# One decoder trunk on one core: later block products and Gram products, later keys in the last head, held sums and fewer table operations in the first head, closer steps in the last scan

## The chip, the core and the metric

The kernel runs on one NeuronCore of a Trainium2 chip. The core has a matrix engine (TensorE, "PE" in the profile, with its weight loads listed apart as "PEld"), a vector engine (VectorE, "DVE"), a scalar engine (ScalarE, "ACT"), a general engine (GpSimd, "POOL") and a queue engine (SyncE, "SP") that only issues transfers. Each engine works through its own instructions in order and waits for the others by semaphores. Transfers (DMA) are issued from the queues of SP, ACT and POOL and run beside the engines. The metric is the time of one execution in microseconds (us).

## The reference

Two residual layers over 512 positions of width 2048, in float32. Layer 0 is gated differential attention (8 heads, two query/key pairs of 128 and a value of 256 each, RMS norm and rotary positions on queries and keys). Layer 1 is an RWKV-7 time mixing with 32 heads of 64.

```python
proj = h @ w_in                                      # layer 0: q, k, v, gate
q = apply_rope(rms_norm(q, q_gain), cos, sin)
k = apply_rope(rms_norm(k, k_gain), cos, sin)
a = softmax(q1 k1) - lam * softmax(q2 k2)            # causal
o = rms_norm(a @ v, subln_w) * (1.0 - lambda_init)
x = x + (o * silu(gate)) @ w_out
...
def step(S, inp):                                    # layer 1: the scan over time
    r_t, w_t, k_t, v_t, a_t, b_t = inp
    sa = jnp.einsum('bhvk,bhk->bhv', S, a_t)
    S = S * w_t[:, :, None, :] + sa[..., None] * b_t[:, :, None, :] + v_t[..., None] * k_t[:, :, None, :]
    y = jnp.einsum('bhvk,bhk->bhv', S, r_t)
    return S, y
```

The result of the scan is normalised per head (group norm), gated and projected back.

## The kernel before

**Products and weights.** Every large product is made of three passes over values that are split in a high part and a low rest (`mm3`, L122 of the listing: high x high, high x low, low x high), each a matmul with 512 moving columns. Weights arrive by DMA in blocks of 512 KB (`wraw`, three buffers). `split_w` turns a block into its high part on ACT (`wh`, L105) and its rest on DVE (`wl`, L106), two buffers each. `split_w` is marked urgent: the compiler's list scheduler, which orders each engine's instructions by their place in the program less an offset and by when it thinks that their inputs are ready, puts it ahead of its place (offset `AHEAD`, 2000). `tc.issue_after(ins)` only orders: what is written under it comes behind `ins` on the same engine.

**Chains.** Small work that has to run between the large matmuls is written as generators in `Chain`. Each `yield n` means: go on after n more of the large matmuls. `tick` is called for each of these and counts only for the first chain of the list; a later chain's count starts when the one before has ended. `finish` runs what is left of a chain at once. A chain's steps have an offset of `SCAN` (3000), the solve one of `SOLVE` (4000).

**Layer 0.** The first head's projections are plain (`unit_tok`: 16 rows of blocks in 8 weight blocks, four token tiles; 192 matmuls). From the second head on, `unit_head` needs fewer products by using sums and differences of quarters of the input. `input_sums` makes these sums for eight pairs of input blocks while the first head runs: nine DVE operations and three ACT operations for each pair (L497, L498, L502, L514, L519, L521), written ahead of the first head's second projection, and a last sum (`late`) behind it. The input pairs lie in buffers that are later used for values, gates and the chained weight blocks `Ta` to `Td`. `rope_tables` builds the tables of cosines and sines with the gains, tile by tile (L221 to L225). `attention` is a chain of a head's scores, softmax, weighted values and output transposes; its first step also transposes the keys and queries of the last two token tiles (`turn_qk`, L296). The last head's chain (`rows` is given then) runs under the output projection, a `unit_tok` whose `all_rows` forces the chain to its end before matmul 150; it starts after 16 matmuls.

**Layer 1.** The heads go in 16 pairs, `for j in range(D // P)`. An iteration makes the value projection of pair j (`proj(2, j)`), the key projection of the next pair, from the fourth iteration on a gate projection of an earlier pair, and the next pair's receptance projection; each `proj` is a `unit_chan` of 48 matmuls. In iteration 1 the gate projection of pair 0 stands in the place of the third. After 18 matmuls of `proj(2, j)`, `behind` issues `gram`: the sums of squared keys (L1335) and the 32 Gram products (L1352), their copies on ACT and stores by SP to `ltd`. `t_solve` loads that back through POOL's queue (`LT`) and solves a triangular system row by row on DVE (L1411, L1413), and SP stores the result (`td<-Tm`). Pairs 0 to 2 are solved in one go, 3 to 14 in parts.

The chain of pair j-1 starts at the head of iteration j. `t_combine` loads the solved blocks (`TT<-td`, SP), waits `lead` matmuls, transposes them on DVE (L1450), 8 matmuls later multiplies them with the Gram blocks (the block products, `px`, L1456), 10 later with the other factor (L1467), and 8 later `scan_pair` begins: eight chunks of 64 positions, each with three products (L1549, L1560, L1567) `gap`, `gap` and `gap_s` matmuls apart, ACT's copies between the first two (L1552, L1562), DVE's state update behind the third (L1571). `outputs` (L1589, L1593) and `centre` end it. The bank of `px` is also that of `stage_v`'s product, which `y` (L1482) reads. The lead is 64 for the first chain, 18 for the second, 42 for the third and 10 after that; the gaps are (4, 5) for pairs 0 and 1, (5, 6) for pair 2, (6, 8) for pairs 3 to 13, (4, 4) for pair 14. `group_norm` of pair j-2 (L1615 to L1621) runs ahead of `proj(2, j)` if that pair's chain has ended (`normed`), and otherwise in `behind`, after `t_solve`; `finish_y` (L1628, L1630) turns its result back.

The last pair's chain starts behind the loop, 24 matmuls after the one before has ended, with lead 24 and gaps (5, 5), under two gate projections and the first columns of the output projection; its group norm and `finish_y` are called at matmul 144 of that.

Of the kernel before, what the change touches and what calls it, by code (L numbers as in the profile page):

```python
# [18 lines left out]
ALU = mybir.AluOpType  # L19
# [4 lines left out]
P = 128  # L24
# [3 lines left out]
NT = T // P  # L28
# [58 lines left out]


@urgent
def split_w(g, parts, kg, cols, k0, raw=None, fine=False, turn=None):  # L90

    nc = g.nc
    if raw is None:
        raw = g.wraw.tile([P, kg, cols], F32, name="wraw", tag="wraw")
        if turn:
            g.fetch(k0, kg)
        load_w(g, raw, parts, k0, slice(0, kg))
    hi = g.wh.tile([P, kg, cols], F32R, name="wh", tag="wh")
    lo = g.wl.tile([P, kg, cols], F32R, name="wl", tag="wl")
    for ks in [slice(k, k + 1) for k in range(kg)] if fine else [slice(0, kg)]:  # L100
        k = k0 + ks.start
        with ExitStack() as after:
            for ins in g.made[-1] if turn and g.made else ():
                after.enter_context(g.tc.issue_after(ins))
            a = nc.scalar.copy(hi[:, ks], raw[:, ks])  # L105
            d = nc.vector.tensor_sub(lo[:, ks], raw[:, ks], hi[:, ks].bitcast(F32))  # L106
        if turn:
            turn(ks.stop - ks.start, a.ins, d.ins)
    return hi, lo


# [4 lines left out]
def vg_cols(aps, h):  # L116
    return aps["da_w_in"], 2 * h + 1
# [43 lines left out]
                c.step(g)  # L161


def unit_tok(g, aH, aL, parts, cols, npp=NT, more=None, late=True, turn=None, behind=None):

    nc = g.nc
    pts = [g.pp.tile([P, 512], F32, name="pp", tag="pp") if npp == NT or t % 3 == 0 else
           g.ps.tile([P, 512], F32, name="pt", tag="pb", bufs=2) for t in range(NT)]
    KG = 1024 // cols
    m = None  # L170
    for k0 in range(0, KT, KG):
        raw, fine = g.first.pop(0) if g.first else (None, False)
        wh, wl = split_w(g, parts, KG, cols, k0, raw, fine, turn)
        by_k = fine or more and late and k0 + KG == KT
        order = [(k, t) for k in range(KG) for t in range(NT)] if by_k else \
                [(k, t) for t in range(NT) for k in range(KG)]
        for i, (k, t) in enumerate(order):
            if more and i in (0, 2, 4):
                more(k0 + (k + 1 + i % 4 // 2 if by_k else KG + i // 2), m)
            kk = k0 + k  # L180
            s = slice(t * P, (t + 1) * P)
            with g.tc.issue_after(behind) if behind and not m else ExitStack():
                m = mm3(nc, pts[t][:, :cols], aH[kk][:, s], aL[kk][:, s], wh[:, k, :], wl[:, k, :],
                        kk == 0, kk == KT - 1, g)
    return pts


def rope_tables(g, aps):
    nc = g.nc
    c = g.lc  # L190
    wide = g.work.tile([P, 4, NT, 64], F32, name="rope", tag="sB2", bufs=1)
    ang, n, sn, cs = [wide[:, i] for i in range(4)]
    rows = g.work.tile([P, 4, P], F32, name="ropein", tag="a", bufs=1)
    pos_i = g.small.tile([P, NT], I32, name="pos_i", tag="mx")
    nc.gpsimd.dma_start(out=pos_i[:], in_=aps["positions"].rearrange("o (t p) -> (o p) t", p=P),)
    pos = g.small.tile([P, NT], F32, name="pos", tag="nb")
    nc.vector.tensor_copy(pos[:], pos_i[:])
# [12 lines left out]
    nc.vector.tensor_scalar(ang[:], ang[:], math.pi, -math.pi, ALU.min, ALU.max)  # L210
    nc.scalar.activation(sn[:], ang[:], AF.Sin)
    nc.scalar.activation(cs[:], ang[:], AF.Sin, scale=0.5)
    nc.vector.tensor_mul(cs[:], cs[:], cs[:])
    nc.vector.tensor_scalar(cs[:], cs[:], -2.0, 1.0, ALU.mult, ALU.add)
    g.C = c.tile([P, NT, 2, P], F32, name="ropeC")
    g.S = c.tile([P, NT, 2, P], F32, name="ropeS")
    for i, nm in enumerate(("da_q_gain", "da_k_gain")):
        gn = rows[:, i]
        nc.gpsimd.dma_start(out=gn[:], in_=aps[nm][0].partition_broadcast(P))
        for t in range(NT):  # L220
            nc.vector.tensor_mul(g.C[:, t, i, 0:64], cs[:, t, :], gn[:, 0:64])  # L221
            nc.vector.tensor_mul(g.C[:, t, i, 64:128], cs[:, t, :], gn[:, 64:128])
            nc.vector.scalar_tensor_tensor(g.S[:, t, i, 0:64], sn[:, t, :], -1.0, gn[:, 64:128],
                                           ALU.mult, ALU.mult)
            nc.vector.tensor_mul(g.S[:, t, i, 64:128], sn[:, t, :], gn[:, 0:64])  # L225


def lambda_full(g, aps):
# [98 lines left out]
def attention(g, h, qkT, qkL, sq, V, VL, G, gap, rows=None, keys=()):  # L327
# [92 lines left out]
    for i in range(NT + 3):  # L420
# [12 lines left out]
        if i < NT:  # L433
            scores(i)
        if i == 0 and keys:
            yield 7
            turn_qk(*keys[0])
            yield 9
            turn_qk(*keys[1], "pc")
            yield max(gap - 28, 6)  # L440
        else:
            yield gap - 12
# [27 lines left out]
KG = 2  # L470


def input_sums(g, pairs, late):
# [34 lines left out]
    for k in range(NH4):  # L508
# [10 lines left out]
        nc.vector.scalar_tensor_tensor(c, c, norm(k + NH4), d, ALU.mult, ALU.add)  # L519
        put("S4", k, c)  # L520
        nc.vector.tensor_sub(a, a, b)  # L521


def first_tiles(g, aps, h):
# [288 lines left out]
def layer0(g, aps):  # L813
# [3 lines left out]
    with ExitStack() as cx:  # L817
# [95 lines left out]
        for h in range(NH):  # L913
# [15 lines left out]
            else:  # L929
                for ts in ([0, 1], [2, 3]):  # L930
                    head_qk(g, t1s, sq, ts)
                Chain(g, keys(2), 120)
                input_sums(g, pairs, False)
                ps = unit_tok(g, g.hH, g.hL, vg_cols(aps, h), 512)
                acc1 = g.work.tile([P, 2, 512], F32, name="acc1", tag="acc1", bufs=1)
                G, vg = gates(g)
                vg += [acc1[:, 0], acc1[:, 1]]
                copy_out(g, vg, ps)
                for c in list(g.chains):
                    c.finish(g)  # L940
                input_sums(g, pairs, True)
                first_tiles(g, aps, 1)
                values = head_vg(g, h, vg, G)
            before = qkT + (sq,) + values
# [688 lines left out]
def layer1(g, aps):  # L1633
    nc, tc = g.nc, g.tc
    with ExitStack() as cx:
# [6 lines left out]
        def proj(i, j, **k):  # L1642
            return unit_chan(g, (aps["rw_w_in"], i * KT + j), P, **k)[0]
# [24 lines left out]
        for j in range(D // P):  # L1668
            p = pairs[j]
            if j:  # L1670
# [7 lines left out]
                if full:  # L1678
                    others += [(4, lambda p=p: next(p.solve)), (6, lambda p=p: (next(p.solve), weigh()))]
                gaps = ((6, 8) if j > LAG + 1 else (5, 6)) if full else (4, 4) if j > LAG else (4, 5)  # L1680
                leads = {1: 64, LAG: 18, LAG + 1: 42}
                chain(g, j - 1, pairs[j - 1], 5, *gaps, others, leads.get(j, GAP_D - GAP_T)).step(g)
            stage2(g, j, r, p)
            normed = j > LAG + 1 and pairs[j - 2].chain.wait is None
# [14 lines left out]
                if j > 1 and not normed:  # L1699
                    group_norm(g, j - 2, pairs[j - 2])  # L1700

            stage_v(g, j, p, proj(2, j, behind=(18, behind)))
            if j == 0:
                turn_keys(g, p, 0)
                turn_keys(g, p, 4)
# [9 lines left out]
            weigh()  # L1715
            if j == LAG:
                gated(g, 0, pairs[0], first)
        chain(g, j, p, 24, 5, 5, lead=24)
        gps = proj(3, j - 1)
        group_norm(g, j - 1, pairs[j - 1])  # L1720
        gts = [gate(g, j - 1, gps)]
# [139 lines left out]
```

## Time and profile before

| | us |
|---|---|
| median of 3 timed runs | 2065.39 |
| lowest and highest | 2064.68, 2065.81 |
| profiled execution, whole | 2068.84 |
| its span, first to last instruction | 2067.1 |
| PE busy in it | 2047.3 |
| DVE, ACT, POOL busy in it | 1608.3, 1136.2, 387.5 |

The page of the profile gives busy times of each engine and the chain of work that ended last. A list of waits says for which instruction of which line an engine stood idle, and what released it; the name of the releaser is that of the last semaphore event by the profile. A table by windows gives, for any stretch of time, the busy time and count of each engine and the mean granted clock of PE as a share of full speed. The order of time lists single instructions: start, duration, engine, line, operation, what is written from what, count, and in brackets the idle time just before, with its releaser.

### The profile page before, as it was taken

The numbers are of one execution on the slowest core, as the hardware profiler recorded it, in microseconds if no ns is written. First come the engines' busy times: TensorE is split into PE (matmuls) and PEld (weight loads), VectorE is DVE, ScalarE is ACT, GpSimd is POOL, SyncE is SP. The second block draws the span as 40 slices with busy tenths as digits, with TensorE's granted clock in tenths as the row PEclk, the third lists the DMA queues.
The fourth block names the chain that finished last, engine by engine and source line by source line (L and its number), as shares of the span: only waits on it lengthen the run. The fifth ranks groups of instructions, "written<-read, shape, count | busy, mean of one in ns | idle before, by whom it ended". The sixth has DMA issues, their size and how long they took to land.

```text
span 2067.1 us, 34180 instructions
## 1 busy us (share of the span) xinstructions
PE 2047.3 (99%) x11922; PEld 1676.8 (81%) x11922; DVE 1608.3 (78%) x4128; ACT 1136.2 (55%) x2262; POOL 387.5 (19%) x774
## 2 busy tenths in 40 slices
PE   9999999999999999999999999999999999999999
PEld 8788888888888888888777778888888888877787
DVE  7988988888898976476777788877777887767745
ACT  5765656565666544365465555555555555545333
POOL 1020111102011000101132322322222222232011
PEclk9999999999999999999999999999999999999999
DMA  8487978879787965823333223233333233346676
GB/s 286 151 163 193 178 173 184 164 192 165 190 178 171 271 215 173 173 86 107 92 85 95 87 86 96 88 95 98 97 97 98 87 95 87 106 129 198 199 191 143
DMA packets 159533, 297.76 MB, mean 144 GB/s; under 512 B 64528, under 2 KB 81936, under 8 KB 159360
## 3 DMA queue, kind: packets, MB, share of 16 engines
q1 hardware_dynamic: 110768, 184.39, 28.7%
q0 software_dynamic: 25952, 90.88, 23.1%
q10 hardware_dynamic: 22640, 20.30, 3.1%
q8 instruction: 94, 1.54, 0.3%
q14 instruction: 79, 0.65, 0.1%
HBM read 271.33 MB, written 24.18 MB: 143 GB/s over the span
## 4 chain that ended last, share of the span: by engine, by line
PE 85%; DVE 9%; ACT 2%; issue 2%; DMA 1%; ACTq 0%; DVEq 0%; SPq 0%
PE pp L122 44%; PE pp L573 22%; PE pt L122 5%; DVE wl L106 2%; PE sm L1549 2%; PE gp L1352 1%; PE sc L122 1%; PE o L122 1%; PE sm L1567 1%; PE sm L1560 1%; ACT wh L105 1%; PE Y L1589 1%; DVE tmpl L1411 1%; PE lora L1094 1%; PE z L122 1%
## 5 line engine op out<-in xcount | busy, mean ns | idle before, releaser
L106 DVE TENSOR_TENSOR wl<-wraw,wh 128x1024 fp32r<-128x1024 f32 (+1 forms) x286 | 350.6, 1226 | 176.4 <-ACT wh L105 169.5
L105 ACT CAST wh<-wraw 128x1024 fp32r<-128x1024 f32 (+1 forms) x286 | 299.4, 1047 | 250.4 <-PE pp L122 124.8
L122 PE MATMUL pp<-hL,wh 128*128 128x512 f32 x1024 | 415.1, 405 | 0.0
L122 PE MATMUL pp<-hH,wh 128*128 128x512 f32 x1024 | 414.0, 404 | 0.4 <-ACT wh L105 0.4
L122 PE MATMUL pp<-hH,wl 128*128 128x512 f32 x1024 | 414.1, 404 | 0.0
L122 PEld LDWEIGHTS pp<-hH,wh 128*128 128x128 f32 x1024 | 193.6, 189 | 35.4 <-ACT wh L105 0.6
L122 PEld LDWEIGHTS pp<-hL,wh 128*128 128x128 f32 x1024 | 193.6, 189 | 33.8
L122 PEld LDWEIGHTS pp<-hH,wl 128*128 128x128 f32 x1024 | 193.8, 189 | 32.4
L573 PE MATMUL pp<-wh,hH 128*128 128x512 f32 x448 | 176.8, 395 | 0.0
L573 PE MATMUL pp<-wh,hL 128*128 128x512 f32 x448 | 175.7, 392 | 0.0
L122 PE MATMUL pp<-wl,hH 128*128 128x512 f32 x376 | 147.8, 393 | 0.9 <-DVE wl L106 0.9
L122 PE MATMUL pp<-wh,hL 128*128 128x512 f32 x376 | 147.5, 392 | 0.0
L122 PE MATMUL pp<-wh,hH 128*128 128x512 f32 x376 | 147.2, 392 | 0.1
L1411 DVE SCALAR_TENSOR_TENSOR tmpl<-LT,Tm 128x60 f32<-128x60 f32 (+24 forms) x496 | 134.4, 271 | 13.3
L573 PE MATMUL pp<-wl,hH 128*128 128x512 f32 x448 | 140.4, 392 | 0.0
L1555 POOL COPY SA<-VS 64x64 f32<-64x64 f32 x224 | 57.0, 254 | 405.3 <-DVE VS L1571 383.4
L1413 DVE TENSOR_TENSOR Tm<-Tm,tmpl 128x60 f32<-128x60 f32 (+24 forms) x496 | 104.2, 210 | 11.7
L1552 ACT COPY rhs<-sm 64x64 f32<-64x64 f32 x256 | 53.0, 207 | 92.2 <-PE sm L1549 89.6
L573 PEld LDWEIGHTS pp<-wl,hH 128*128 128x128 f32 x448 | 84.4, 188 | 17.2
L573 PEld LDWEIGHTS pp<-wh,hH 128*128 128x128 f32 x448 | 84.2, 188 | 17.3 <-issue 0.3
L573 PEld LDWEIGHTS pp<-wh,hL 128*128 128x128 f32 x448 | 84.2, 188 | 16.3
L1562 ACT COPY VS<-sm 64x64 f32<-64x64 f32 x256 | 52.9, 207 | 72.9 <-PE sm L1560 66.4
(432 smaller groups left out, 4378.1 us busy)
## 6 DMA issues: line engine op xcount, KB each, us to landing
wraw<-in_rw_w_in_dram SPq DMA_DIRECT2D x128, 512.0 KB
wraw<-in_da_w_in_dram SPq DMA_DIRECT2D x75, 512.0 KB
wraw<-in_da_w_in_dram POOLq DMA_DIRECT2D x28, 512.0 KB, 6.5
wraw<-in_da_w_out_dram SPq DMA_DIRECT2D x26, 512.0 KB
wraw<-in_rw_w_out_dram SPq DMA_DIRECT2D x24, 512.0 KB
Ta<-in_da_w_in_dram POOLq DMA_DIRECT2D x21, 512.0 KB, 5.6
Tb<-in_da_w_in_dram POOLq DMA_DIRECT2D x21, 512.0 KB, 5.7
Tc<-in_da_w_in_dram POOLq DMA_DIRECT2D x21, 512.0 KB, 5.5
```

The source lines that it names most:

```text
L105: a = nc.scalar.copy(hi[:, ks], raw[:, ks])
L106: d = nc.vector.tensor_sub(lo[:, ks], raw[:, ks], hi[:, ks].bitcast(F32))
L122: m = nc.tensor.matmul(out, a, b, start=s, stop=e, skip_group_check=skip)
L573: m = nc.tensor.matmul(out[t][:], x, wt[lo][:, k, :], start=first, stop=end and lo == 1 and k == KG - 1, skip_group_check=True)
L1094: m = nc.tensor.matmul(pts[i][:, s], wt[:, c : c + P], x[k][:, s], start=k == 0 and s.start == 0 and c < 2 * P and x is g.hH, stop=k == KT ...
L1352: m = nc.tensor.matmul(gp[h][:, i * P : (i + 1) * P], BK[r_, c0 + i, :, :], p.AR[r_, c0 + i, :, :], start=True, stop=True)
L1411: nc.vector.scalar_tensor_tensor(tt, LT[:, i : i + 1, i + 1 :].to_broadcast([P, s, n]), n2[:, i : i + 1], Tm[:, 0:s, i : i + 1].to_broadca ...
L1413: nc.vector.tensor_add(Tm[:, 0:s, i + 1 :], Tm[:, 0:s, i + 1 :], tt)
L1549: nc.tensor.matmul(sm[:, 0:P], both(p.G[:, c, 0]), both(VS[:, c]), start=True, stop=True)
L1552: nc.scalar.copy(rhs[r_, :], sm[r_, h * C : h * C + C])
L1555: nc.gpsimd.tensor_copy(p.SA[r_, c - 1, :], VS[r_, c, h, :])
L1562: g.copied = nc.scalar.copy(VS[r_, c, h, :], sm[r_, P : P + C])
```

## The change

Six edits, none of which alters what is computed.

1. In the first head, `input_sums` becomes a generator that stops after each pair. Three pairs are issued where all eight were; the others one by one, each behind the two split operations of a weight block of the second projection (`also`), with an offset that takes that of `split_w` back.
2. `rope_tables` works on four token tiles at once, with the gains broadcast: 8 operations of 256 columns in place of 32 of 64.
3. In the last head, the transposes of the keys and queries of the third tile come 12 matmuls after the first scores, not 7.
4. The second pair's `behind`, and so its Gram products, comes after 24 matmuls of `proj(2, 1)`, not 18.
5. The first chain's lead is 72, not 64.
6. The last chain's lead is 34, not 24, and its gaps are (4, 5), not (5, 5).

```diff
-def split_w(g, parts, kg, cols, k0, raw=None, fine=False, turn=None):
+def split_w(g, parts, kg, cols, k0, raw=None, fine=False, turn=None, also=None):
...
+    if also:
+        also(a.ins, d.ins)
     return hi, lo
...
-        for t in range(NT):
-            nc.vector.tensor_mul(g.C[:, t, i, 0:64], cs[:, t, :], gn[:, 0:64])
-            nc.vector.tensor_mul(g.C[:, t, i, 64:128], cs[:, t, :], gn[:, 64:128])
-            nc.vector.scalar_tensor_tensor(g.S[:, t, i, 0:64], sn[:, t, :], -1.0, gn[:, 64:128],
-                                           ALU.mult, ALU.mult)
-            nc.vector.tensor_mul(g.S[:, t, i, 64:128], sn[:, t, :], gn[:, 0:64])
+        lo, hi = [gn[:, None, c0 : c0 + 64].to_broadcast([P, NT, 64]) for c0 in (0, 64)]
+        nc.vector.tensor_mul(g.C[:, :, i, 0:64], cs[:], lo)
+        nc.vector.tensor_mul(g.C[:, :, i, 64:128], cs[:], hi)
+        nc.vector.scalar_tensor_tensor(g.S[:, :, i, 0:64], sn[:], -1.0, hi, ALU.mult, ALU.mult)
+        nc.vector.tensor_mul(g.S[:, :, i, 64:128], sn[:], lo)
...
         if i == 0 and keys:
-            yield 7
+            yield 7 if rows is None else 12
             turn_qk(*keys[0])
...
         put("S4", k, c)
         nc.vector.tensor_sub(a, a, b)
+        yield
...
-                input_sums(g, pairs, False)
-                ps = unit_tok(g, g.hH, g.hL, vg_cols(aps, h), 512)
+                early = input_sums(g, pairs, False)
+                for _ in range(3):
+                    next(early)
+
+                def also(a, d):
+                    with tc.high_priority(offset=-AHEAD), tc.issue_after(a), tc.issue_after(d):
+                        next(early, None)
+
+                ps = unit_tok(g, g.hH, g.hL, vg_cols(aps, h), 512, also=also)
...
-                leads = {1: 64, LAG: 18, LAG + 1: 42}
+                leads = {1: 72, LAG: 18, LAG + 1: 42}
...
-            stage_v(g, j, p, proj(2, j, behind=(18, behind)))
+            stage_v(g, j, p, proj(2, j, behind=(24 if j == 1 else 18, behind)))
...
-        chain(g, j, p, 24, 5, 5, lead=24)
+        chain(g, j, p, 24, 4, 5, lead=34)
```

`unit_tok` passes `also` on to `split_w`; the late sums are drawn from the generator in a loop that does nothing else.

More of the change, by code (lines that the diff above doesn't have):

```diff
@@ L161, in tick, with unit_tok @@
                 c.step(g)
-def unit_tok(g, aH, aL, parts, cols, npp=NT, more=None, late=True, turn=None, behind=None):
+def unit_tok(g, aH, aL, parts, cols, npp=NT, more=None, late=True, turn=None, behind=None, also=None):
     nc = g.nc
@@ L172, in unit_tok @@
         raw, fine = g.first.pop(0) if g.first else (None, False)
-        wh, wl = split_w(g, parts, KG, cols, k0, raw, fine, turn)
+        wh, wl = split_w(g, parts, KG, cols, k0, raw, fine, turn, also)
         by_k = fine or more and late and k0 + KG == KT
@@ L940, in layer0 @@
                     c.finish(g)
-                input_sums(g, pairs, True)
+                for _ in input_sums(g, pairs, True):
+                    pass
                 first_tiles(g, aps, 1)
```

## The prediction

> **What bounds the kernel now.** I read the page first, then the list of what TensorE (PE) waits for, then the granted clock in narrow windows, and last the order of time around each wait. The page:
>
> ```profile
> span 2067.1 us, 34180 instructions
> ...
> PE 2047.3 (99%) x11922; PEld 1676.8 (81%) x11922; DVE 1608.3 (78%) x4128; ACT 1136.2 (55%) x2262; POOL 387.5 (19%) x774
> ```
>
> PE is the bound: of 2067.1 us only 19.8 are idle. The change removes no matmul, so it can win only idle time of PE, or time in which PE runs slowly. The waits (total us, times, longest):
>
> ```profile
> PE sm L1549 <- DVE VS L1571: 3.2, 8, 0.9
> ...
> PE px L1456 <- DVE y L1482: 1.6, 1, 1.6
> PE px L1456 <- DVE T L1450: 1.3, 1, 1.3
> PE gp L1352 <- DVE AR L1325: 1.0, 1, 1.0
> PE pp L122 <- DVE wl L106: 0.9, 1, 0.9
> PE pt L296 <- ACT t L281: 0.7, 1, 0.7
> ...
> PE pt L1628 <- DVE yc L1621: 0.3, 1, 0.3
> ```
>
> Each of the last six is one wait, and each has an edit. The second thing to see is the clock, next to last in each row of this table by windows (after it DMA share and GB/s):
>
> ```profile
> 1011.30:1014.72 3.42, 1.86 (x38) 1.31 (x37) 1.93 (x4) 1.40 (x2) 2.22 (x5) 1.00 0.28 90
> 1014.72:1018.13 3.41, 3.41 (x16) 2.23 (x17) 2.04 (x4) 2.23 (x5) 2.54 (x2) 0.50 0.55 143
> 1878.30:1881.70 3.40, 2.08 (x36) 1.55 (x37) 3.30 (x7) 3.36 (x7) 0.00 (x0) 1.00 0.78 283
> 1881.70:1885.11 3.41, 3.41 (x39) 2.41 (x38) 3.40 (x8) 2.61 (x6) 0.00 (x0) 0.50 0.79 231
> 1147.80:1151.20 3.40, 2.47 (x12) 1.80 (x11) 3.27 (x10) 1.32 (x4) 0.96 (x3) 1.00 0.36 111
> ```
>
> Right behind the waits of 1.6 and 1.3 us comes a stretch of 3.41 us at half clock; PE was busy 1.86 and 2.08 us in the stretch before. With 2.47 us busy (a wait of 0.9) none follows. Two rows of the chain of waits price it:
>
> ```profile
> 766.12 71.67 PE pp L122 x316
> ...
> 1014.04 3.95 PE pp L122 x10
> ```
>
> One matmul of 512 columns takes 71.67/316 = 0.227 us, at half clock 0.395: ten of them lose 1.68 us. Two stretches are 3.36 us.
>
> **The change, part by part.** First head: sums and tables. The order of time on VectorE (DVE) and on ScalarE (ACT):
>
> ```profile
> 45.79 0.22 DVE L222 TENSOR_TENSOR ropeC<-rope,ropein 128x64 f32<-128x64 f32 x1
> ...
> 49.95 0.42 DVE L270 TENSOR_TENSOR t<-t,ropeS 128x256 f32<-128x256 f32 x1
> ...
> 54.94 0.61 DVE L514 TENSOR_SCALAR pair<-pair,norms 128x256 f32<-128x256 f32 x2
> ...
> 56.26 1.22 DVE L106 TENSOR_TENSOR wl<-wraw,wh 128x1024 fp32r<-128x1024 f32 x1
> ```
> ```profile
> 51.52 1.05 ACT L105 CAST wh<-wraw 128x1024 fp32r<-128x1024 f32 x1
> ```
>
> The high part of this weight block was cast by 52.57, yet its low part started at 56.26, behind sums; PE waited 0.9 for it. 32 table operations of 64 columns (0.22 each, 7.0 in all by their durations, less by their starts, as they overlap) become 8 of 256. The broadcast form is not there; the row with the same shape and a broadcast table costs 0.42, so 3.4 us. I take half of the difference, 1.8 us, as won on DVE. The sums from 54.94 on (1.3 us) belong to pairs from the fourth on, now issued behind later weight blocks. 1.8 + 1.3 is over 0.9: **gain 0.9** (0 to 0.9, if other work fills the place). The held sums fall where DVE has idle time, and the work in total shrinks.
>
> Last head's keys, 5 matmuls later (5 x 0.227 = 1.13 us):
>
> ```profile
> 728.69 1.27 ACT L281 ACTIVATE t<-t,rr 128x128 f32<-128x128 f32 x4
> ```
>
> The keys are scaled by ACT from 728.69 on, and the transposes stood 0.7 us for them. 1.13 covers it: **gain 0.7** (0.3 to 0.7). The chain of this attention has no spare step: 16+12+7+9+6+5x20 = 150 matmuls, and it is forced to its end at matmul 150 of the output projection. So its last output transposes can come at most as late as now; 18 matmuls (4.1 us) stand between them and the rows that need them, which hides a shift of 1.1. Without that cover the loss is 1.1 - 0.7 = 0.4, so the lower end.
>
> Second pair's Gram at matmul 24 instead of 18, and the first pair's block products 8 later. In order of time (PE, ACT, DVE, the chain, PE):
>
> ```profile
> 996.78 2.06 PE L1352 MATMUL gp<-AR,BK 64*128 64x128 f32 x32 [1.02 <-DVE AR L1325]
> ```
> ```profile
> 1000.34 1.06 ACT L105 CAST wh<-wraw 128x1024 fp32r<-128x1024 f32 x1
> ```
> ```profile
> 1003.67 1.22 DVE L106 TENSOR_TENSOR wl<-wraw,wh 128x1024 fp32r<-128x1024 f32 x1
> ```
> ```profile
> 1003.82 2.18 DMA td<-Tm
> ...
> 1006.07 4.93 DMA TT<-td
> ...
> 1011.03 0.44 DVE T L1450
> ```
> ```profile
> 1013.34 0.69 PE L1456 MATMUL px<-T,G 32*32 32x32 f32 x32 [1.56 <-DVE y L1482]
> ```
>
> Gram: 6 x 0.227 = 1.36 covers 1.02: **gain 1.0** (0.8 to 1.0). What it issues later is 0.3 us later (1.36 - 1.02): copies, masks on GpSimd (POOL), the stores on SP's queue, and the second solve, which is not waited for soon. Block products: PE wanted them at 1013.34 - 1.56 = 1011.78; it will want them 8 x 0.227 = 1.81 later and 1.02 earlier, at 1012.57. Their inputs do not come from PE: the solve is stored, loaded back, transposed by DVE, and they share a bank with y. If nothing of that moves they start at 1013.34 and the wait is 0.8: **gain 0.8**. Bounds: 1.6 if DVE takes y before the transposes; -0.4 if the solve ends 1.2 later. The latter can be: the weight block cast at 1000.34 waited for a buffer freed by matmul 24, now free before the Gram; its low part (1.22), which ran behind the solve, can fall into it. I take the middle value, as the projection's end, and so y, comes 1.0 earlier too. A wait of 0.8 is below the 0.9 that left the clock alone.
>
> Last pair's block products 10 later:
>
> ```profile
> 1878.06 0.75 DVE L1179 SCALAR_TENSOR_TENSOR mixv<-pp,mu,mixv 128x511 f32<-128x511 f32 x1
> ...
> 1879.52 0.44 DVE L1450 STREAM_TRANSPOSE T<-TT 64x256 f32<-64x256 f32 x1
> ```
> ```profile
> 1880.01 0.69 PE L1456 MATMUL px<-T,G 32*32 32x32 f32 x30 [1.32 <-DVE T L1450]
> ```
>
> The second transpose sat behind a gate's mix. Ten matmuls are 2.27 us against a wait of 1.32: **gain 1.3** (0.6, if one more weight operation of 1.23 and a row split slip in front of it).
>
> Closer steps in the last scan. Waits within the last scan, then within the second pair's scan, which has the new gaps (4, 4, 5) already:
>
> ```profile
> PE sm L1549 <- DVE VS L1571: 0.3, 1, 0.3
> ```
> ```profile
> PE sm L1549 <- DVE VS L1571: 0.8, 3, 0.5
> ```
>
> So 0.5 more. Against that the scan is 7x13+8 = 99 instead of 115 matmuls and ends 6 earlier, 1.4 us, which ends the 0.3 wait for yc: **loss 0.2** (from a gain of 0.3 to a loss of 1.0).
>
> What is late next: an iteration of the loop over pairs has 192 matmuls in its projections, 144 in the third. The first chain took 64+8+10+8+99 = 189 of 192; now 197, five into the next. The second then starts five later and ends at 5+18+8+10+8+99 = 148 of 144, four over; the third at 4+42+8+10+8+122 = 194 of 192. So at the fifth iteration the third pair's scan has not ended, and its group norm moves behind the Gram; the fourth chain takes the shift up. All waits of those scans together:
>
> ```profile
> PE sm L1549 <- DVE VS L1571: 2.1, 5, 0.9
> ```
>
> They will be dealt anew; I take 0 (1 either way, half of them).
>
> **The sum.** 0.9 + 0.7 + 1.0 + 0.8 + 1.3 - 0.2 = 4.5 us of waits, and up to 3.36 of slow clock. In the profiled execution: span 2067.1 - 4.5 - 3.4 = 2059.2. That execution took 2068.84 us, 1.7 around its span and 3.45 above the median of 2065.39, about what its two slow stretches cost; whether a timed run has them I cannot see. The two stretches start 866.98 us apart, 254.0 times 3.413: they lie on a grid, and a wait of 1.3 to 1.6 falls whole into one a little over half of the time. I count one per timed run: 2065.4 - 4.5 - 1.7 = **2059.2 us**.
>
> [...]
>
> **The rivals.** (1) The slow stretches are not won: timed runs have none, or something else causes them. For it: the profiled run's 3.45 us over the median. Against: each follows one of the two longest waits inside the program. 2065.4 - 4.5 = 2060.9. (2) Every timed run has both: 2065.4 - 4.5 - 3.4 = 2057.5. For it: the timed runs lie within 1.1 us of each other, less than one stretch. (3) The first pair's wait stays, as the solve ends 1.2 later (1013.34 + 1.2 - 1012.57 = 2.0, so -0.4 instead of +0.8), its stretch stays too, and the last scan loses 1.0 instead of 0.2: 4.5 - 1.2 - 0.8 = 2.5 and half of the other stretch, 0.8: 2062.1. Against: y comes earlier. (4) Slower: the third pair's group norm, now traced behind a solve that has priority.
>
> ```profile
> 1178.37 0.69 DVE L1621 TENSOR_TENSOR yc<-yc,rsg 128x512 f32<-128x512 f32 x1
> ...
> 1192.16 0.18 DVE L1400 TENSOR_SCALAR LT<-LT 128x32 f32<-128x32 f32 x1
> ...
> 1209.56 0.23 DVE L1413 TENSOR_TENSOR Tm<-Tm,tmpl 128x66 f32<-128x66 f32 x1
> ```
> ```profile
> 1183.26 0.60 PE L1628 MATMUL pt<-ident,yc 128*128 128x128 f32 x4
> ```
>
> If its last operation slips past 1192.16, the solve's first part runs before it, to 1209.8; the transposes at 1183.26 stand in PE's queue until 1210.5: 27.2 lost, 6.2 won, 2086.4. It decides from 13.1 us of slip on (1192.16 - 1179.06). For it: the priorities. Against: the scan ends only 0.5 us later (2 matmuls past the boundary), and DVE is free between 1179 and 1192 save for weights and steps.
>
> **Chances.** Forecast 0.42; (1) 0.20; (2) 0.13; (3) 0.13; (4) 0.12. 0.2% is 4.1 us, about what a measurement of this kernel can tell from no change; faster means below 2061.3. The forecast is there 9 times in 10, (1) a little over half, (2) always, (3) one in four: 0.38 + 0.12 + 0.13 + 0.03, about 0.66. Slower is (4), 0.12; the rest, 0.22, is no change. Range 2055.2 to 2064.3: below, both stretches won and the better bounds (2057.5 less 0.8 + 0.5 + 1.0); above, (3) with a loss of 1 in the early scans, its other stretch not won (0.8) and the keys at their lower end (0.4).
>
> **What would show it.** PE's waits for wl L106 at 57, for t L281 at 728 and AR L1325 at 996 are gone; px L1456 waits at most 0.8 in the first pair and not in the last; no window at half clock between 900 and 1950; yc L1621 is not waited for; L1549, L1560 and L1567 wait about 0.5 more in the last scan. I am wrong if px of the first pair still waits over 1.2, if a wait at L1628 near 1180 appears, or if PE's idle time falls by less than 3 us.

## The result, and the profile after

The changed kernel took **2060.6 us** (median of 15 runs, 2059.52 to 2063.42), the kernel before on the same chip 2065.39 (15 runs, 2064.24 to 2069.2). The ratio is 0.9978, with a 95% interval of 0.9971 to 0.9985. The profiled execution took 2061.87 us, its span 2060.2. The prediction was 2059.2 (2055.2 to 2064.3).

The page of the changed kernel, and its list of waits (us in total, times, longest):

```profile
span 2060.2 us, 34171 instructions
...
PE 2041.7 (99%) x11922; PEld 1675.0 (81%) x11922; DVE 1608.8 (78%) x4104; ACT 1135.5 (55%) x2262; POOL 385.2 (19%) x774
```
```profile
PE sm L1559 <- DVE VS L1581: 3.1, 6, 0.9
...
PE pt L1638 <- DVE yc L1631: 1.8, 2, 1.5
PE px L1466 <- DVE T L1460: 1.0, 1, 1.0
PE sm L1570 <- ACT rhs L1562: 1.0, 2, 0.8
```

(From the second layer on, lines have moved by 10: L1466 was L1456, L1638 was L1628.) The waits for `wl`, for the scaled keys at 728, for `AR` and both px waits of the prediction are gone. Yet PE's idle time fell from 19.8 us (2067.1 - 2047.3) to 18.5 only, not by 4.5: a px wait of 1.0 and one of 1.5 for the group norm (`yc`) are new, and the scans wait at L1570 too. The rest of the 6.9 us of span, 5.6, is time in which PE counts as busy (2047.3 - 2041.7). By the prediction's price 3.4 of that is the two half-clock stretches; 2.2 is neither listed wait nor clock. The span and mean granted clock of the profiled execution, before and after (one stretch would make it 0.999):

```profile
core 0: 2067.1 us, clock 0.998
core 0: 2060.2 us, clock 1.000
```

So the first comparison raised three questions. Do the timed runs of the kernel before have the half-clock stretches that its one profile showed? Where do the new waits come from? And does listed idle time measure what a wait costs?

### The profile page after: what moved, and what is told of

It reads as the page before. It is cut to its first block, busy times and chain, and to the rows that moved or that the text cites. A ratio compares the mean times of both kernels' runs of the same rounds, so it can differ in the third digit from the quotient of the medians.

```text
span 2060.2 us, 34171 instructions
## 1 busy us (share of the span) xinstructions
PE 2041.7 (99%) x11922; PEld 1675.0 (81%) x11922; DVE 1608.8 (78%) x4104; ACT 1135.5 (55%) x2262; POOL 385.2 (19%) x774
## 4 chain that ended last, share of the span: by engine, by line
PE 88%; DVE 7%; ACT 3%; issue 1%; DMA 1%; ACTq 0%; SPq 0%; DVEq 0%
PE pp L124 45%; PE pp L575 23%; PE pt L124 5%; DVE wl L106 2%; PE gp L1362 2%; PE sc L124 1%; PE sm L1559 1%; PE o L124 1%; PE sm L1577 1%; PE sm L1570 1%; ACT wh L105 1%; PE Y L1599 1%; PE lora L1104 1%; PE pt L297 1%; PE z L124 1%
```

## The experiments

Each kernel ran 11 times, with 33 runs of the kernel before in each group of four on one chip. The medians of the kernel before were 2066.38 (first group), 2064.97 (second) and 2065.46 (third). Every run came with its span and its mean granted clock, so a stretch at half clock, which takes 1.7 of some 2064 us, shows as 0.999, two as 0.998. Below, "at full clock" means the runs that show 1.0. The edits are given against the kernel named.

**The kernel before, again (no edit).**

> The kernel before, unchanged; every one of its runs comes with its span and its mean granted clock, which the first measurement did not give. Theory: the two half-clock stretches behind the two px waits are in the timed runs too; a stretch of 3.41 us at half clock takes 0.0008 off the mean over 2064 us, so most runs should show 0.999 (one stretch) or 0.998 (two), and the runs with the lower clock the longer spans, by about 1.7 us for each stretch. Rival: the stretches belong to the one profiled execution; then nearly all runs show 1.0, and the 4.8 us that the change won are waits alone.

2065.19 us, ratio 0.9999 (0.999 to 1.0008). Its profile has a span of 2063.1 and no stretch at half clock until PE's last matmul has ended; the wait of the first pair's block products was a third of that in the first profile, since the solved block came back from memory sooner. In order of time, DVE and PE:

```profile
1009.72 0.44 DVE L1450 STREAM_TRANSPOSE T<-TT 64x256 f32<-64x256 f32 x1 [1.78 <-DMA TT<-td]
...
1011.45 0.69 DVE L1482 TENSOR_TENSOR y<-pt,mixv 128x512 f32<-128x512 f32 x1
...
1012.20 0.69 PE L1456 MATMUL px<-T,G 32*32 32x32 f32 x32 [0.50 <-DVE y L1482]
```

The transpose began at 1009.72, in the first profile at 1011.03, while the last operation of the solve (L1420) ended within 0.1 us of the same time. The 1.56 on which the prediction rested is one draw of a transfer whose end lay 1.3 us apart in these two. In the three later profiles with a lead of 64 (last pair, first layer, tables alone) the wait is 0.4 to 0.6, so the 1.56 is the odd one of five. Of the runs, 3 of 11 had a mean clock of 0.999. Theory and rival are both half right. Over all runs that list a clock (mean spans in us):

| instructions | runs | clock 1.0: runs, mean span | below 1.0: runs, mean span |
|---|---|---|---|
| kernel before (4 sets) | 110 | 74, 2063.3 | 36, 2065.2 |
| changed kernel (3 sets) | 37 | 34, 2059.5 | 3, 2062.7 |

Without the stretches the change wins 2063.3 - 2059.5 = 3.8 us; the clock adds the difference of what each loses by it on average, 36/110 x 1.9 - 3/37 x 3.2 = 0.62 - 0.26, about 0.4. Both are averages over groups that differ. Of the 33 runs of the kernel before, 18 were below a clock of 1.0 in the first group, 4 in the second and 11 in the third; in the second group, the only one with the changed kernel beside it, the change won 3.5 us at full clock and nothing by the clock (4 of 33 against 3 of 22). In the first comparison the runs of the kernel before list no clock.

**The first and second pair's parts alone.** Against the kernel before:

```diff
-                leads = {1: 64, LAG: 18, LAG + 1: 42}
+                leads = {1: 72, LAG: 18, LAG + 1: 42}
...
-            stage_v(g, j, p, proj(2, j, behind=(18, behind)))
+            stage_v(g, j, p, proj(2, j, behind=(24 if j == 1 else 18, behind)))
```

> Only the first pair's block products 8 matmuls later (lead 72) and the second pair's Gram after 24 matmuls. Theory: the waits AR of 1.0 and px of 1.6 go and the half-clock stretch near 1015 goes with them, the one near 1882 stays; but the first chain runs 5 matmuls over its iteration, so the waits come back further on: the early scans wait about 3.8 instead of 2.6 us and px of the fifth pair 1.0 near 1230. Idle time falls by under 0.6 us, and the time by that and a share of 1.7 us: 2063.2 to 2065. Rival: the waits that the changed kernel has near 1036 to 1230 come from the first layer's edits, which shift everything by 0.9 us; then they are not here, idle time falls by 2.4 us, and the time is 2061.5 to 2063.

2062.97 us, ratio 0.9984 (0.9976 to 0.9993); all 11 runs at a clock of 1.0. The waits are those that the theory named: `AR` and the first px wait gone, px of the fifth pair 0.9, L1549 and L1560 4.6 together, 3.8 of it in the early scans. Idle time rose from 18.7 to 19.7, 0.8 of which is the start of the program. By idle time nothing was won; yet the runs have a mean span of 2061.0, against 2063.5 for those of the kernel before at full clock in this group. The median lies under the theory's range and just inside the rival's, though the waits are the theory's.

**The last pair alone.** Against the kernel before:

```diff
-        chain(g, j, p, 24, 5, 5, lead=24)
+        chain(g, j, p, 24, 4, 5, lead=34)
```

> Only the last pair: lead 34 and gaps (4, 5). Theory: the px wait of 1.3 near 1880 goes, and the stretch at half clock behind it; the group norm of the pair before is now what PE meets first, with about 1.5 us at L1628; idle time stays within 0.4 us of before, and the time falls by a share of 1.7 us: 2063.7 to 2065.4. Rival: the wait for the group norm in the changed kernel comes from what was moved further ahead; then L1628 waits at most 0.3, idle time falls by 1.3 us, and the time is 2062.4 to 2064.1.

2064.62 us, ratio 0.9995 (0.9986 to 1.0004), as the theory said: the last pair's px does not wait, L1628 waits 1.1, L1560 behind the last scan's first product 0.6. At full clock the mean span is 0.5 under the kernel before, no more than the noise. All 11 runs are at a clock of 1.0 here too, though the first pair's px still waits 0.6; in the run before this one it was the last pair's that still waited, 1.1. Either edit alone left no stretch, so these runs do not tell which of the two waits brings the stretches of the timed runs.

**The first layer's edits alone** (held sums, table operations, keys; the second layer as before).

> Only the first layer's edits: sums held, 8 table operations in place of 32, keys of the last head 5 matmuls later. Theory: the waits of 0.9 near 57 and 0.7 near 728 go, some 0.2 to 0.7 us of new waits come up in the attention of other heads, both px waits (1.6 and 1.3) and their stretches stay: 2064.3 to 2064.9. Rival: a shift of 0.9 us is enough to re-deal the waits of the second layer; then their sum differs from before by over 1 us, and a stretch is missing.

2063.86 us, ratio 0.9989 (0.998 to 0.9998). Both waits went, one of 0.2 came, and 4 of 11 runs are below a clock of 1.0. The second layer's waits are those that the kernel before has in its second profile. Against its first profile the px waits are 1.5 us less and both stretches are missing, as the rival asked; but the kernel before differs as much from itself, so this does not speak for the rival. At full clock the runs are 2.1 us under the kernel before, more than expected. The three parts alone have 2.5, 0.5 and 2.1, together 5.1, where the whole has 3.5 to 3.8; with 7 to 11 runs each the difference is at the edge of the noise, so whether they simply add stays open.

**The changed kernel, again (no edit).**

> The changed kernel again, as the anchor for the next three on the same chip. Both theories: 2060 to 2061.5, all runs at a mean clock of 1.0, px of the fifth pair waits about 1.0 near 1229, the group norm at L1638 about 1.5 near 1878 in its profile.

2061.75 us, ratio 0.9983 (0.9974 to 0.9992). The median is a little above the range. px of the fifth pair waits 1.0; at the last pair the 1.5 is split, 1.1 at L1638 and 1.2 at L1570.

**The second chain inside its iteration.** Against the changed kernel:

```diff
-                leads = {1: 72, LAG: 18, LAG + 1: 42}
+                leads = {1: 72, LAG: 13, LAG + 1: 42}
```

> The changed kernel with lead 13 in place of 18 for the second chain, so that it ends inside its iteration again. Theory (lateness): the first chain's 5 matmuls of excess go no further; the scans of the second and third pair wait about 1.8 us together as in the kernel before (in the changed one 2.3) and px of the fifth pair does not wait near 1229; PE idles 1.0 to 1.8 us less than in the changed kernel, which is 0.5 to 1.8 us faster. Rival: the waits are dealt by chance of placement, whatever the iteration; then px of the fifth pair still waits 0.8 or more, or a like wait turns up elsewhere, and the idle time is the same within 0.5 us.

2062.22 us, ratio 0.9984 (0.9976 to 0.9993): not faster. The waits did what the theory said. px of the fifth pair does not wait, the two scans have 1.6 together, and idle time fell from 18.9 to 17.0. But runs at full clock took a mean span of 2060.3 against 2059.8. How far PE really got is read from the same product in each kernel. Here a view of one line in a stretch (count, then durations of one in ns, then first start and last end): the first product behind the first layer, and the sixth iteration's Gram. First the kernel before (its second profile), then the changed kernel, then lead 13:

```profile
L1094 PE MATMUL lora<-hH,wh x6: 278/282/283, 900.6 to 901.5; 128*128 128x256 f32 x6
L1352 PE MATMUL gp<-AR,BK x32: 272/272/373, 1291.7 to 1293.4; 64*128 64x128 f32 x32
```
```profile
L1104 PE MATMUL lora<-hH,wh x7: 277/283/364, 899.8 to 902.9; 128*128 128x256 f32 x7
L1362 PE MATMUL gp<-AR,BK x32: 272/272/373, 1289.6 to 1291.4; 64*128 64x128 f32 x32
```
```profile
L1104 PE MATMUL lora<-hH,wh x10: 277/283/384, 898.8 to 902.9; 128*128 128x256 f32 x10
L1362 PE MATMUL gp<-AR,BK x32: 272/272/373, 1289.9 to 1291.7; 64*128 64x128 f32 x32
```

Between the two lie 391.1 us before, 389.8 in the changed kernel, and 391.1 again with lead 13. The lateness that brought the listed waits is also where the gain lies. A scan of the third pair in the run with lead 13 shows how both can be true, in order of time on PE and, for the second place, its weight load (PEld):

```profile
1148.19 0.39 PE L124 MATMUL pp<-hH,wh 128*128 128x512 f32 x1
1148.42 0.38 PE L1577 MATMUL sm<-VS,BKT 128*128 128x128 f32 x2
1148.56 0.47 PE L124 MATMUL pp<-hL,wh 128*128 128x512 f32 x1
...
1152.73 0.39 PE L124 MATMUL pp<-hL,wh 128*128 128x512 f32 x1
1153.10 0.30 PEld L1577 LDWEIGHTS sm<-VS,BKT 128*128 128x128 f32 x2 [0.41 <-ACT VS L1572]
1153.10 0.49 PE L1577 MATMUL sm<-VS,BKT 128*128 128x128 f32 x2
1153.35 0.48 PE L124 MATMUL pp<-hH,wl 128*128 128x512 f32 x1
```

Large matmuls start 0.23 apart, but each is drawn 0.39 long. The first small pair was ready: from the large matmul ahead of it to the one behind it 0.37 us. The second took 0.62: its weights waited for ACT's copy. Neither matmul has an idle time in brackets, since the time lost lies under the drawn end of the matmul ahead. A late input here costs 0.25 us that counts as busy, and a scan has three small products in each of its eight chunks. So the busy share of PE does not tell in these rows how far it got: a matmul is drawn 0.39 us long and takes up 0.23.

From such rows the stretches of each profile can be laid side by side (us; the third column runs to the transposes of pair 13, L1628 or L1638, the fourth to the end of the span; times are good to about 0.1). A star marks a column that holds a stretch at half clock, worth 1.7:

| profile | first layer | five pairs | middle | last pair and end | PE idle |
|---|---|---|---|---|---|
| before, first | 900.7 | 393.4* | 538.8 | 234.2* | 19.8 |
| before, second | 900.6 | 391.1 | 538.8 | 232.6 | 18.7 |
| first and second pair | 900.8 | 389.6 | 538.7 | 232.3 | 19.7 |
| last pair | 900.3 | 391.2 | 538.7 | 232.5 | 19.8 |
| first layer | 898.9 | 390.9 | 538.4 | 232.2 | 17.0 |
| changed | 899.8 | 389.8 | 538.4 | 232.2 | 18.5 |
| changed, second | 899.7 | 389.3 | 538.4 | 232.8 | 18.9 |
| changed, third (below) | 899.7 | 389.9 | 538.4 | 232.5 | 18.4 |
| lead 13 | 898.8 | 391.1 | 538.4 | 232.1 | 17.0 |
| both (lead 13; below) | 898.6 | 390.5 | 538.6 | 232.2 | 16.7 |
| transposes moved (below) | 898.7 | 389.5 | 538.4 | 234.8* | 18.0 |
| the same, gaps (5, 5) (below) | 899.1 | 390.0 | 538.3 | 231.5 | 16.8 |
| tables alone (below) | 899.9 | 390.9 | 538.3 | 234.2* | 18.0 |

The five pairs' stretch took 389.3 to 390.0 us in the six profiles with the edits of the first and second pair as they stand, 390.5 and 391.1 with lead 13 added, and 390.9 to 391.2 in the four with a lead of 64 and full clock there. Summed from each large matmul's start to the next, the places in it with a scan product between take 62.7 to 63.4 us in five profiles of the late order and 63.2 and 63.6 with lead 13, so the scans hold about 0.5 us of a difference of 1.2; the rest lies elsewhere.

**The last pair but one's transposes later.** Against the changed kernel:

```diff
-        gts.append(gate(g, j, proj(3, j, behind=(15, last_but_one)), "E"))
+        gts.append(gate(g, j, proj(3, j, behind=(24, last_but_one)), "E"))
```

> The changed kernel with the transposes of the last pair but one 9 matmuls (2.0 us) later. Theory: the 1.5 us at L1638 near 1878 is the px wait of before come back in front of the group norm's last operation, and 2.0 us cover it: the wait goes, idle time falls by 1.1 to 1.5 us, and the time by 0.5 to 1.5 us. Rival: the next thing behind it, the split of the gated rows or the output projection's first rows, is late in its turn and takes up over half of it.

2061.7 us, ratio 0.9984 (0.9976 to 0.9993). The edit changed nothing: every engine has its instructions in the order of the changed kernel, because the transposes already ran later than matmul 24 of that projection. The run is a third set of the changed kernel, and 3 of its 11 runs were below a clock of 1.0.

**Both of these edits**, so in effect lead 13 once more.

> Both edits. Theory: they add up, idle time falls by 2.0 to 3.2 us against the changed kernel, time 2057.5 to 2059.5. Rival: less than one of them shows.

2061.98 us, ratio 0.9984 (0.9975 to 0.9993), idle time 16.7, five pairs in 390.5: the second reading of lead 13, again with less idle time and no gain. At full clock, the 21 runs with lead 13 are 0.45 us slower than the 19 of the changed kernel beside them (95% interval 0.1 to 0.8), where by their idle time they would have been some 1.8 us faster.

**Block products of the first pair earlier.** Against the kernel before:

```diff
-                leads = {1: 64, LAG: 18, LAG + 1: 42}
+                leads = {1: 56, LAG: 18, LAG + 1: 42}
```

> The kernel before with the first pair's block products 8 matmuls earlier (lead 56): the px wait near 1010 becomes 2.3 to 3.4 us (0.5 to 1.6 plus 8 x 0.227). Theory: a stretch of 3.41 us in which PE stood idle for some 1.3 us or more is followed by one at half clock; a wait of 2.3 cannot avoid that but in a few alignments, so 9 or more of 11 runs show a mean clock of 0.999 or lower, the profile shows a half-clock row behind the wait, and the time rises by 1.8 and 1.6 us: 2068 to 2070. [...]

2068.75 us, ratio 1.0016 (1.0007 to 1.0025). Of 11 runs, 10 are below a clock of 1.0, four of them at 0.998. The profile, by windows (length, busy us and count of PE, its weight loads, DVE, ACT and POOL, then the granted clock):

```profile
1008.73:1012.15 3.42, 1.51 (x35) 1.01 (x35) 2.20 (x4) 0.52 (x1) 1.30 (x3) 1.00 0.55 170
1012.15:1015.56 3.41, 3.41 (x21) 2.67 (x15) 0.00 (x0) 2.39 (x6) 2.43 (x4) 0.50 0.53 154
```

The px wait was 1.9 us, less than the 2.3 expected. The theory holds in its main point for this place: the wait of 1.9 us, far below the 3.41 us of a stretch, has half clock behind it in the profile, and 10 of 11 runs are below a clock of 1.0, where the kernel before has 11 of 33 in the same group. As a rule for any wait with 1.3 us of idle time or more it does not hold; the last section has windows with 1.5 and 1.6 us idle and full clock behind them.

**The transposes really moved.** Against the changed kernel, `last_but_one` is called from the output projection's rows:

```diff
-        gts.append(gate(g, j, proj(3, j, behind=(15, last_but_one)), "E"))
+        gts.append(gate(g, j, proj(3, j), "E"))
+        waiting = [last_but_one]
...
-        def all_rows(n, _):
+        def all_rows(n, m):
+            if m is not None and waiting:
+                waiting.pop()(m)
```

> The changed kernel with the transposes of the last pair but one called from the output projection's rows, which puts them 8 matmuls and the second block products later on PE (about 2.6 us). Theory: the wait at L1638 near 1878 (1.1 to 1.6) goes and nothing of its size follows, the last stage is 0.8 to 1.6 us shorter, and the time 0.5 to 1.5 us under the changed kernel's 2061.7. Rival: the copies behind the last scan's first product (L1570 from ACT, 1.0 to 1.2 in two of the profiles) take its place, and under 0.5 us is won.

2062.3 us, ratio 0.9984 (0.9975 to 0.9992). The rival won: the wait at L1638 near 1878 went, and the copies behind the last scan's first product held PE for 2.0 us, with half clock behind it. ACT, then PE:

```profile
1881.02 1.14 ACT L452 CAST hH<-yr 128x512 fp32r<-128x512 f32 x2
1882.06 0.62 ACT L1521 ACTIVATE thg<-mixE 128x512 f32<-128x512 f32 x1
1882.60 0.60 ACT L452 CAST hH<-yr 128x512 fp32r<-128x512 f32 x1
1883.22 0.43 ACT L1562 COPY rhs<-sm 64x64 f32<-64x64 f32 x2
...
1883.70 0.43 PE L1570 MATMUL sm<-rhs,TT 128*128 128x64 f32 x2 [2.01 <-ACT rhs L1562]
```

The small copy stood behind row casts of the output projection. While PE stood at L1638 the casts went on, so that wait had covered this one (in the second profile of the changed kernel they share the time, 1.1 and 1.2).

**The same, with gaps (5, 5) in the last scan.**

```diff
-        chain(g, j, p, 24, 4, 5, lead=34)
+        chain(g, j, p, 24, 5, 5, lead=34)
```

> The same, and the last scan with gaps (5, 5) as before. Theory: any wait at L1570 near 1884 falls by 0.2, the other steps of the last scan have the waits of the kernel before, the scan ends 8 matmuls later and the group norm behind it is waited for as before (0.3): within 0.5 us of the run without this edit, so that the closer steps are worth nothing either way. Rival: the closer steps cost what the prediction's lower bound said, 1.0 us, and this run is 0.7 us or more faster than that without.

2060.93 us, ratio 0.998 (0.9971 to 0.9988). The wait at L1570 fell from 2.0 to 1.0 and the last stretch from 234.8 to 231.5 us, the shortest of all; 1.7 of this is the half clock that the other profile had there. At full clock its runs have a mean span of 2059.1, those without the edit 2059.7: nearly the rival's 0.7, and more than the 0.2 of the prediction. But with 8 and 6 runs the 95% interval of this difference reaches from 1.4 faster to 0.2 slower, so it is likely and not shown that the closer steps cost. Against the changed kernel's 2061.7 it is 0.8 lower, but the two intervals overlap nearly in whole; a version that beats the changed kernel was not shown.

**The table operations alone** (the 8 in place of 32; sums, keys and the second layer as before).

> The kernel before with the 8 table operations in place of 32 alone. Theory: they win 1.8 us on DVE ahead of the weight block's low part, so the wait of 0.9 near 57 goes without the held sums; time 0.7 to 1.2 us under before. Rival: the sums decide, the low part still runs behind them, and 0.4 us or more of that wait stay.

2064.4 us, ratio 0.9992 (0.9984 to 1.0001). Of the wait of 0.9, 0.3 stayed. DVE in this kernel, then in the changed one:

```profile
54.69 0.86 DVE L501 SCALAR_TENSOR_TENSOR pair<-pair,norms 128x256 f32<-128x256 f32 x2
55.48 1.21 DVE L106 TENSOR_TENSOR wl<-wraw,wh 128x1024 fp32r<-128x1024 f32 x1
```
```profile
41.86 0.42 DVE L224 TENSOR_TENSOR ropeC<-rope,ropein 128x256 f32<-128x256 f32 x1
...
53.04 1.22 DVE L106 TENSOR_TENSOR wl<-wraw,wh 128x1024 fp32r<-128x1024 f32 x1
```

The low part started at 56.26 before, at 55.48 with the tables alone and at 53.04 with the sums held as well. The time lies in the theory's range, but neither theory nor rival has the mechanism: the tables win two thirds of the wait, the sums the rest, with 2.4 us in hand.

## Why the prediction was right, and where it was not

The direction and the range were right, and the time was 1.4 us too low. The forecast was 4.5 us of waits and 1.7 of clock; the timed runs gave about 3.8 and 0.4 (the medians on record differ by 4.8; in the one group that has both kernels, 3.2 and 3.3).

**The clock term** failed in "I count one per timed run". The profiled execution had two stretches; only a third of the timed runs of the kernel before had one, none in 110 showed two, and the share went from 4 of 33 in one group to 18 of 33 in another. The spacing on which I counted is that of one profile: its granted clock falls at 1014.72, at 1881.70 and, after PE's last matmul, at 2066.02 us, and the 866.98 and 184.32 between are 254 and 54 times 3.413. The "little over half of the time" was my estimate from this and from waits of 1.3 to 1.6 us. No run shows that share, and it would have needed the waits of the profile, 1.56 and 1.32, in every run; in the second profile they were 0.50 and 1.10. That half clock can follow a wait much shorter than 3.41 us was right, as lead 56 showed: the wait was 1.9 us, and PE was busy for 1.51 of 3.42 us in the window ahead of half clock. The rival of 2060.9 still came nearest to 2060.6: there were few stretches to win, whatever made them.

**First layer, 1.6.** Both waits went. With these edits alone the first layer ended 1.7 earlier, in three profiles of the changed kernel 0.8 to 0.9; over all eight profiles that have them it ended at 898.6 to 899.8, against 900.3 to 900.8 in the five without them, so on average about 1.4 earlier. It varies because small waits of other heads' attention come and go between executions (0.2 at 257 and 0.5 at 682 in the changed kernel's first profile, 0.7 at 435 in its second). Of the terms, "half of the difference, 1.8 us, as won on DVE" was too much: the tables moved the low part by 0.8. The broadcast operation costs 0.42 as taken from the other row; the held sums covered the shortfall.

**Second pair's Gram and first pair's block products, 1.0 and 0.8.** Against the second profile of the kernel before, the five pairs' stretch is 1.2 to 1.8 shorter in the changed kernel, 1.5 with this part alone, near the 1.8. That is in part luck: in that profile the two waits are only 1.0 and 0.5, and new ones of 1.0 at px and 0.8 at L1570 came up in the same stretch, so its listed waits did not fall in total. What was won there lies in time that counts as busy. The upper bound, "if DVE takes y before the transposes", is what happened, at least before the second of them, and nothing is left of the wait. Most of that is the draw of the transfer again: in the second profile of the kernel before, the block products began at 1012.20 as it was, ahead of the 1012.57 at which the prediction has PE want them. DVE, then PE in the changed kernel:

```profile
1009.30 0.44 DVE L1460 STREAM_TRANSPOSE T<-TT 64x256 f32<-64x256 f32 x1 [3.19 <-DMA TT<-td]
...
1010.47 0.69 DVE L1492 TENSOR_TENSOR y<-pt,mixv 128x512 f32<-128x512 f32 x1
...
1011.19 0.44 DVE L1460 STREAM_TRANSPOSE T<-TT 64x256 f32<-64x256 f32 x1
...
1011.62 0.76 PE L1466 MATMUL px<-T,G 32*32 32x32 f32 x32
```

**What is late next** was traced rightly (5, 4 and 2 matmuls over) but not followed to its place. With the third chain late, the fifth pair's block is called for where a weight operation and a receptance mix stand ahead of its second transpose, just what the last pair's edit was to cure:

```profile
1227.31 1.18 DVE L106 TENSOR_TENSOR wl<-wraw,wh 128x1024 fp32r<-128x1024 f32 x1
1228.41 0.73 DVE L1189 SCALAR_TENSOR_TENSOR mixr<-pp,mu,mixr 128x511 f32<-128x511 f32 x1
1229.18 0.44 DVE L1460 STREAM_TRANSPOSE T<-TT 64x256 f32<-64x256 f32 x1
...
1229.67 0.69 PE L1466 MATMUL px<-T,G 32*32 32x32 f32 x30 [1.04 <-DVE T L1460]
```

The run with lead 13 showed that lateness makes this wait, and also that taking it away wins nothing. Why the late order takes less time is not settled. The wait at L1628 of the fourth rival did not come.

**Last pair, 1.3 less 0.2.** This failed: its stretch is 232.2 to 232.8 against 232.6, and alone 232.5. "Ten matmuls are 2.27 us against a wait of 1.32" took the wait away, but two more stood behind it. In the kernel before (second profile), and in the changed one:

```profile
1877.36 0.69 PE L1456 MATMUL px<-T,G 32*32 32x32 f32 x30 [1.10 <-DVE T L1450]
...
1881.66 0.60 PE L1628 MATMUL pt<-ident,yc 128*128 128x128 f32 x4
```
```profile
1875.38 0.69 PE L1466 MATMUL px<-T,G 32*32 32x32 f32 x32
...
1879.20 0.63 PE L1638 MATMUL pt<-ident,yc 128*128 128x128 f32 x4 [1.54 <-DVE yc L1631]
```

The group norm of the pair before has its operations interleaved with row splits on DVE, and while PE stood at px they went on. I named the end of the last pair's own group norm as what comes next, not this one. Behind it stood the scan's copies on ACT.

**The signs.** Right: the four waits, px, the clock. Wrong: "yc L1621 is not waited for" (1.5 and 0.3); "L1549, L1560 and L1567 wait about 0.5 more in the last scan" (in the changed kernel's first profile that scan has no wait at all, in its second one of 1.2, at ACT's copy); and "PE's idle time falls by less than 3 us", which I had given as a proof against me. It fell by 1.3, and the kernel was faster all the same, since idle time does not hold all of a wait.

## What to carry to other kernels

Take a wait's size from more than one execution where a transfer stands behind it (here 1.56 us in one, 0.50 in the next), and ask of each wait what is ready just after it: at two of the three places here a new wait came up further on, and at one of them, the last pair, nearly all of the gain went into it. Judge an edit by when the same later instruction starts, not by the sum of listed waits. In these profiles, where a large matmul is drawn 0.39 us long and the next starts 0.23 us after it, a product that came 0.25 us late showed no idle time.

## What the runs showed of the hardware

Of the 14 profiles, ten have a mean granted clock of 1.000, two of 0.999 (tables alone, transposes moved) and two of 0.998 (the first of the kernel before, lead 56): six stretches of 3.41 us at half clock inside the program. Two of them by windows, each behind the stretch ahead of it, from the run with the tables alone and the one with the transposes moved, and beside them a wait of 1.6 us that had no such effect (both edits, lead 13 once more):

```profile
1873.46:1876.87 3.41, 2.17 (x37) 1.38 (x37) 3.14 (x6) 3.41 (x6) 0.00 (x0) 1.00 0.78 205
1876.87:1880.29 3.42, 3.42 (x9) 2.33 (x8) 3.42 (x9) 3.23 (x7) 0.00 (x0) 0.50 0.87 252
```
```profile
1880.85:1884.26 3.41, 1.40 (x8) 0.88 (x6) 3.23 (x6) 3.33 (x8) 0.00 (x0) 1.00 0.70 213
1884.26:1887.68 3.42, 3.42 (x11) 2.75 (x10) 2.77 (x6) 1.07 (x4) 0.91 (x3) 0.50 0.82 231
```
```profile
1876.69:1880.11 3.42, 1.80 (x11) 1.14 (x9) 3.42 (x9) 3.31 (x7) 0.00 (x0) 1.00 0.86 261
1880.11:1883.52 3.41, 3.41 (x46) 2.79 (x45) 3.41 (x6) 3.35 (x7) 0.00 (x0) 1.00 0.90 317
```

PE busy for 2.17 us was followed by half clock, busy for 1.80 was not. One difference is what it was busy with. In the first of these windows 0.93 us of PE's time are the block products, which use tiles of 32 by 32 (the same window for that tile alone):

```profile
1873.46:1876.87 3.41, 0.93 (x32) 0.71 (x32) 0.00 (x0) 1.00 0.78 205
```

Less the block products, PE has 1.01 to 1.40 us of work in five windows that half clock follows: 1.16 and 1.40 in the first profile of the kernel before (1.85 and 2.09, of which 0.69 each), 1.01 with lead 56 (1.51, of which 0.50), 1.24 with the tables alone and 1.40 with the transposes moved, where the window holds no block products. It has 1.50 to 1.87 in three that full clock follows: 1.50 with the transposes moved, from 1225.49 to 1228.90 (2.30, of which 0.80), 1.80 with both edits and 1.87 in the changed kernel, from 1876.95 to 1880.36, the last two without block products. Four of the five stretches came behind waits at the block products (1.56, 1.32, 1.9 and 1.2 us), the fifth behind the longest wait of all, 2.0 us at L1570. These are eight windows, and no run was made to test what sets them apart; why the clock fell behind some and not behind others is not shown.
